# Masked softmax of a matmul: mask loaded ahead of W, zero fills on VectorE, row spread from the identity on ScalarE, TensorE busy on zeros until data lands

## The chip, the cores and the metric

The kernel runs on one core of one Trainium2 chip. The metric is the time of one execution on the device, in microseconds (us). The profile's span is shorter, because it runs from the first to the last instruction. How much shorter depends on the kernel: 1.8 us for the changed kernel (1.75 to 1.85 in its four runs), but 2.3 for the kernel before (median of 97 later runs, 2.18 to 2.47). So some 0.5 us of any difference between these two lies outside the span, where no profile shows its cause.

"Granted clock" is the share of full speed that TensorE was allowed, as the profile records it. x0, x1 and so on are the inputs of units 0, 1 and so on.

The records call a run "slow" when it is over 1.5% above the fastest run of the same kernel. Here that label is about time alone: among the later runs of the kernel before, one took 94.12 us at a mean granted clock of 0.973 and is called slow, another took 91.67 us at 0.972 and is called fast. The clock does not separate them. The profiled run of this kernel is a slow one (94.61 us, clock 0.957). The spread of the kernel before turns out to be part of the story.

## The reference

```python
batch, m, k, n = 16, 512, 512, 512
x = randn(batch, m, k); weight = randn(k, n); scale = 0.125      # float32
mask = (np.triu(np.ones((m, n))) == 0)                           # strictly lower triangle, as float32

y = scale * np.matmul(x, weight)
y = np.where(mask == 1, y, -1e9)
return softmax(y, axis=-1)
```

## The kernel before

Sixteen units of work, each of 1 MB of x in and 1 MB of output. A unit holds one half (upper or lower 256 rows) of two batches, four rows per partition. For each unit VectorE casts x to bf16, TensorE transposes it, VectorE and ScalarE bring the transposes back from PSUM, TensorE multiplies with W and adds a mask bias (`band`) through the identity, ScalarE takes the exponential with row sums, VectorE divides, and SyncE stores. For the upper half only 256 columns are computed, since the rest is masked; those output halves are filled once with constants.

The opening, which the change touches, prepares what all units use: W in bf16, the identity, the output fills, and the band, which is made from the diagonal blocks of the mask with a matrix `spread` that gives each mask row its place among the partitions.

```python
    load(0)                                               # 1 MB on SyncE's DMA queue
    seq(nc.sync.dma_start(w_f32, weight...))              # 1 MB
    seq(nc.sync.dma_start(diag_f32, diag_r))              # 0.26 MB in rows of 512 bytes
    for u in range(1, X_BUFS):                            # X_BUFS = 8
        load(u)
    make_identity(nc, ident_bf)                           # GpSimd
    nc.gpsimd.memset(spread, 0.0)
    # ... eight affine_selects on GpSimd set its ones ...
    # ... two memsets of band on GpSimd ...
    for i in range(0, OUT_BUFS, 2):
        nc.gpsimd.memset(ots[i][:, :, HB:], 0.0)          # 128 x 1024 float32 each
        nc.gpsimd.memset(ots[i][0:2, 0, HB:], 1.0 / N)
    cast(0); transpose(0); evict(0)
    # W: four casts of 128x512, two on VectorE, two on ScalarE
    # diag_bf = mask bias from diag_f32 (VectorE)
    # for t in range(4): matmul(spread, diag_bf), two copies into band (VectorE, ScalarE)
    cast(1)
    for u in range(U + 1):
        # transpose(u+1), cast(u+2), evict(u+1), multiply(u), normalise(u-1), store(u-1)
        # and then, behind that store in the same queue, load(u-1+X_BUFS)
```

All loads and stores go through one DMA queue, in this order. TensorE's program has the transposes of x1 ahead of the first multiply.

The softmax here doesn't subtract the row's maximum and nothing guards it: scores larger than these inputs give would overflow.

## Time and profile before

| | before |
|---|---|
| time, first comparison | 93.98 us median of 4 runs (93.84 to 94.58) |
| span of the profiled run | 92.3 us |
| TensorE / VectorE / ScalarE / GpSimd busy | 75 / 65 / 59 / 17% |
| DMA queue | 34.87 MB, 92.7% of 16 engines' span |
| steady TensorE work | 16.85 to 81.9 us |
| first store / last store issued | 25.63 / 84.57 us |

The page, the chain of waits and the windows of this kernel stand in the prediction below. One more view is useful: the groups of instructions, kept apart by shape. A line gives source line, engine, operation, what it writes and reads with shapes, number of instructions, then busy us and mean ns of one, then idle time before them.

```profile
L83 DVE CAST xb<-xf 128x2048 bf16<-128x2048 f32 x16 | 20.2, 1270 | 8.5 <-DMA xf<-in_x_dram 8.5
...
L185 POOL MEMSET ot<- 128x1024 f32 x4 | 4.6, 1185 | 0.1
...
L193 DVE CAST w_bf<-w_f 128x512 bf16<-128x512 f32 x2 | 3.1, 1612 | 0.0
```

A cast of W with 512 columns took 1612 ns, more than a cast of x with four times as many. The four large fills on GpSimd (POOL, named `ot`) ran beside it.

### The profile page before, as it was taken

How to read it: one execution, taken by the hardware profiler on the slowest of the kernel's cores; microseconds unless marked ns; L12 is line 12 of the kernel's file. 1: busy time of each engine (PE TensorE's matmuls, PEld its weight loads, DVE VectorE, ACT ScalarE, POOL GpSimd, SP SyncE). 2: the span in 40 equal slices, each digit the busy share in tenths (PEclk: the TensorE clock that was granted, in tenths of full speed). 3: DMA queues.
4: the chain of work that ended last, by engine and by line, in shares of the span. 5: the costliest groups of instructions: out<-in, count | busy, mean ns of one | idle time of the engine just before them, and what ended most of it. 6: DMA issues, size and time to landing. Idle time of an engine off the chain costs nothing.

```text
span 92.3 us, 1608 instructions
## 1 busy us (share of the span) xinstructions
PE 68.8 (75%) x580; PEld 48.7 (53%) x580; DVE 60.0 (65%) x119; ACT 54.4 (59%) x151; POOL 15.9 (17%) x33
## 2 busy tenths in 40 slices
PE   0005225699999999999999999999999999940000
PEld 0005100677659857956975885796598577510000
DVE  0045979950857995995999599599395977616000
ACT  5000716064868777977877788797787879650000
POOL 7999960000100010010001001000100010100000
PEclk9999999999999999999999999999999999997555
DMA  0889999999999999999999999999999999999930
GB/s 32 334 309 309 387 430 423 437 415 430 419 419 312 405 426 291 323 423 415 415 433 426 423 430 412 430 419 433 423 430 426 423 423 433 423 426 423 394 156 11
DMA packets 5670, 34.95 MB, mean 379 GB/s; under 512 B 544, under 2 KB 1056, under 8 KB 1568
## 3 DMA queue, kind: packets, MB, share of 16 engines
q1 hardware_dynamic: 5664, 34.87, 92.7%
q8 instruction: 4, 0.07, 0.3%
q14 instruction: 2, 0.02, 0.0%
HBM read 18.09 MB, written 16.78 MB: 378 GB/s over the span
## 4 chain that ended last, share of the span: by engine, by line
PE 72%; DVE 12%; DMA 5%; ACT 1%; DVEq 0%; issue 0%; ACTq 0%
PE py L116 47%; PE pt L92 17%; PE py L125 8%; DMA xf<-in_x_dram 5%; DVE xb L83 3%; DVE w_bf L193 3%; DVE band L216 2%; DVE ot L152 1%; DVE xt L102 1%; PE py L209 1%; ACT ot L135 1%; DVE diag_bf L197 1%; DVEq L263 0%; DVE rinv L150 0%; ACTq L263 0%
## 5 line engine op out<-in xcount | busy, mean ns | idle before, releaser
L116 PE MATMUL py<-w_bf,xt 128*128 128x256 bf16 (+1 forms) x256 | 51.4, 335 | 0.0
L135 ACT ACTIVATE ot<-py 128x256 f32<-128x256 f32 (+1 forms) x64 | 31.2, 493 | 9.3 <-PE py L125 9.1
L116 PEld LDWEIGHTS <-xt 128*128 128x128 bf16 x256 | 25.3, 101 | 12.6
L83 DVE CAST xb<-xf 128x2048 bf16<-128x2048 f32 x16 | 20.2, 1270 | 8.5 <-DMA xf<-in_x_dram 8.5
L92 PE MATMUL pt<-ident_bf,xb 128*128 128x128 bf16 x256 | 18.6, 231 | 9.6 <-DVE xb L83 9.6
L103 ACT COPY xt<-pt 128x1024 bf16<-128x1024 bf16 x16 | 16.2, 1012 | 15.5 <-PE pt L92 11.2
L152 DVE TENSOR_SCALAR ot<-ot,rinv 128x256 f32<-128x256 f32 (+1 forms) x64 | 23.5, 430 | 0.8
L92 PEld LDWEIGHTS <-xb 128*128 128x128 bf16 x256 | 17.0, 104 | 11.6 <-DVE xb L83 10.5
L102 DVE COPY xt<-pt 128x1024 bf16<-128x1024 bf16 x16 | 11.0, 689 | 11.3 <-PE pt L92 11.3
L125 PE MATMUL py<-band,ident_bf 128*128 128x256 bf16 x64 | 18.0, 282 | 0.0
L154 POOL MEMSET ot<- 2x256 f32 x8 | 3.6, 449 | 63.1 <-DVE ot L152 63.1
L135 ACT ACTIVATION_READ_ACCUMULATOR ot<-py 128x1 f32 x64 | 12.8, 200 | 0.0
L125 PEld LDWEIGHTS <-ident_bf 128*128 128x128 bf16 x64 | 6.5, 101 | 4.3
L150 DVE RECIPROCAL rinv<-rsum 128x4 f32<-128x4 f32 x16 | 2.7, 169 | 3.2 <-ACT ot L135 3.2
L185 POOL MEMSET ot<- 128x1024 f32 x4 | 4.6, 1185 | 0.1
L209 PE MATMUL py<-diag_bf,spread 128*128 128x512 bf16 x4 | 1.9, 620 | 3.5 <-DVE diag_bf L197 3.5
L173 POOL TENSOR_SCALAR_AFFINE_SELECT spread<-spread 128x64 bf16<-128x64 bf16 x8 | 3.2, 438 | 0.0
L193 DVE CAST w_bf<-w_f 128x512 bf16<-128x512 f32 x2 | 3.1, 1612 | 0.0
L216 ACT CAST band<-py 64x256 bf16<-64x256 f32 x4 | 1.5, 368 | 2.7 <-DVE band L216 2.5
L209 PEld LDWEIGHTS <-spread 128*128 128x128 bf16 x4 | 0.5, 136 | 4.2 <-POOL ot L186 3.7
L216 DVE CAST band<-py 64x256 bf16<-64x256 f32 x4 | 1.7, 416 | 0.7 <-PE py L209 0.7
L103 ACT ACT_TABLE_LOAD x1 | 1.3, 1283 | 0.7 <-PEq L249 0.7
(12 smaller groups left out, 6.8 us busy)
## 6 DMA issues: line engine op xcount, KB each, us to landing
xf<-in_x_dram SPq DMA_DIRECT2D x16, 1024.0 KB, 14.1
out_dram<-ot SPq DMA_DIRECT2D x16, 1024.0 KB, 11.0
w_f<-in_weight_dram SPq DMA_DIRECT2D x1, 1024.0 KB, 7.6
diag_f<-in_mask_dram SPq DMA_DIRECT2D x1, 256.0 KB, 8.3
```

Of the source, the lines that this page charges most:

```text
L83: seq(nc.vector.tensor_copy(xb, st_x.pop(u)))
L92: nc.tensor.transpose(st_pt[u][kt // 2][:, kt % 2, t], xb[:, t, kt * P : (kt + 1) * P], ident_bf,)
L102: seq(nc.vector.tensor_copy(xt[:, 0:2], pt[0]))
L103: seq(nc.scalar.copy(xt[:, 2:4], pt[1]))
L116: nc.tensor.matmul(py[:, :NC], lhsT=xt[:, kt, t], rhs=w_bf[:, kt, :NC], start=(kt == 0), stop=(kt == KT - 1),)
L125: nc.tensor.matmul(py[:, h * HB : NC], lhsT=ident_bf, rhs=band[:, h, t], start=False, stop=True, skip_group_check=True,)
L135: nc.scalar.activation(out=ot[:, t, :NC], in_=py[:, :NC], func=AF.Exp, bias=0.0, scale=float(scale), accum_out=rsum[:, t : t + 1],)
L152: seq(nc.vector.tensor_scalar_mul(ot[:, t, :NC], ot[:, t, :NC], rinv[:, t : t + 1]))
L154: seq(nc.gpsimd.memset(ot[0:2, 0, :HB], 1.0 / N))
L185: nc.gpsimd.memset(ots[i][:, :, HB:], 0.0)
L193: seq(nc.vector.tensor_copy(w_bf[:, kt], w_f32[:, kt]))
L216: seq(copy(band[half, :, t, g * P : (g + 1) * P], src[half, :, g]))
```

## The change

The intent is a shorter opening: the mask lands early so that its chain of small steps runs while W is still on its way, GpSimd is relieved of the fills and the row spread, and TensorE is kept at work on zeros so that its clock is up when data lands.

```diff
     load(0)
+    seq(nc.sync.dma_start(diag_f32, diag_r))
     seq(nc.sync.dma_start(w_f32, weight...))
-    seq(nc.sync.dma_start(diag_f32, diag_r))
 ...
+    nc.vector.memset(zeros, 0.0)
+    idle = psum_y.tile([P, N], FP32, name="py")
+    for _ in range(WARM):                                  # WARM = 12
+        seq(nc.tensor.matmul(idle, lhsT=zeros[:, :P], rhs=zeros, start=True, stop=True))
     make_identity(nc, ident_bf)
-    nc.gpsimd.memset(spread, 0.0)
-    # eight affine_selects on GpSimd
 ...
-        nc.gpsimd.memset(ots[i][:, :, HB:], 0.0)
+        nc.vector.memset(ots[i][:, :, HB:], 0.0)
 ...
+    # four ScalarE copies of 128x128: spread from ident_bf
     cast(0)
-    transpose(0); evict(0)
-    # four casts of W
     # diag_bf (VectorE)
+    transpose(0); evict(0)
     # spread matmuls and band copies
+    seq(nc.vector.tensor_copy(w_bf[:, 0:2], w_f32[:, 0:2]))
+    seq(nc.scalar.copy(w_bf[:, 2:4], w_f32[:, 2:4]))
     cast(1)
```

More of the change, by code (lines that the diff above doesn't have):

```diff
@@ L17 @@
 OUT_BUFS = 8
+WARM = 12
 @with_exitstack
@@ L69 @@
     spread = const.tile([P, T, P], BF16, name="spread")
+    zeros = const.tile([P, N], BF16, name="zeros")
     band = const.tile([P, 2, T, HB], BF16, name="band")
@@ L161 @@
     load(0)
+    seq(nc.sync.dma_start(diag_f32, diag_r))
     seq(nc.sync.dma_start(w_f32, weight.rearrange("(kt p) n -> p kt n", p=P)))
-    seq(nc.sync.dma_start(diag_f32, diag_r))
     for u in range(1, X_BUFS):
         load(u)
+    nc.vector.memset(zeros, 0.0)
+    idle = psum_y.tile([P, N], FP32, name="py")
+    for _ in range(WARM):
+        seq(nc.tensor.matmul(idle, lhsT=zeros[:, :P], rhs=zeros, start=True, stop=True))
     make_identity(nc, ident_bf)
-    nc.gpsimd.memset(spread, 0.0)
-    for t in range(T):
-        for g in range(2):
-            nc.gpsimd.affine_select(
-                out=spread[:, t, g * HP : (g + 1) * HP].rearrange("k (p e) -> k p e", e=2),
-                in_=spread[:, t, g * HP : (g + 1) * HP].rearrange("k (p e) -> k p e", e=2),
-                pattern=[[-4, HP // 2], [0, 2]],
-                base=-t,
-                channel_multiplier=1,
-                compare_op=ALU.not_equal,
-                fill=1.0,
-            )
     nc.gpsimd.memset(band[:HP, :, :, P:], MASK_NEG)
@@ L184 @@
     for i in range(0, OUT_BUFS, 2):
-        nc.gpsimd.memset(ots[i][:, :, HB:], 0.0)
+        nc.vector.memset(ots[i][:, :, HB:], 0.0)
         nc.gpsimd.memset(ots[i][0:2, 0, HB:], 1.0 / N)
-    cast(0)
-    transpose(0)
-    evict(0)
-    for kt in range(KT):
-        if kt % 2 == 0:
-            seq(nc.vector.tensor_copy(w_bf[:, kt], w_f32[:, kt]))
-        else:
-            seq(nc.scalar.copy(w_bf[:, kt], w_f32[:, kt]))
+    for g in range(2):
+        for e in range(2):
+            seq(
+                nc.scalar.copy(
+                    spread.rearrange("k t (g p e) -> k t g p e", g=2, e=2)[:, :, g, :, e],
+                    ident_bf.rearrange("k (p t) -> k t p", t=T),
+                )
+            )
+    cast(0)
     seq(
@@ L205 @@
     )
+    transpose(0)
+    evict(0)
     for t in range(T):
```

## The prediction

> **What bounds the kernel now.** I read the page first. No compute engine is busy for more than 75% of the span, but the DMA engines are full almost from the first microseconds to the end:
>
> ```profile
> span 92.3 us, 1608 instructions
> ...
> PE   0005225699999999999999999999999999940000
> ...
> DMA  0889999999999999999999999999999999999930
> ```
>
> So there are two long resources: TensorE, without a hole from about 17 to 82 us, and the DMA queue. Next I read the chain of waits in order of time (start, length, what):
>
> ```profile
> 5.82 2.07 DVE xb L83
> ...
> 9.70 3.06 DVE w_bf L193 x2
> ...
> 15.66 1.14 DVE xb L83
> ...
> 16.85 1.89 PE pt L92 x16
> ...
> 21.94 0.85 PE py L116 x4
> ...
> 23.88 0.86 PE py L116 x4
> ```
>
> From 5.8 to 16.85 us the chain is preparation, nearly all on VectorE: cast of x0, casts of W, mask bias, band, cast of x1. From there TensorE runs unbroken, but four matmuls of 256 columns take 0.85 us before 22.8 us, and four of 512 columns take 0.86 after: TensorE does its first 6 us at half speed. Third come windows of 1 us (busy time of PE, PEld, DVE, ACT and POOL, granted clock, DMA share, GB/s):
>
> ```profile
> 28.00:29.00 1.00, 1.00 (x17) 0.95 (x15) 0.74 (x2) 0.74 (x3) 0.00 (x0) 1.00 0.91 328
> 29.00:30.00 1.00, 1.00 (x11) 0.90 (x10) 0.96 (x4) 1.00 (x3) 0.00 (x0) 1.00 1.14 270
> ...
> 35.00:36.00 1.00, 1.00 (x14) 0.75 (x13) 0.00 (x1) 0.72 (x3) 0.00 (x0) 1.00 0.89 213
> ...
> 84.00:85.00 1.00, 0.00 (x0) 0.00 (x0) 0.54 (x2) 0.00 (x0) 0.00 (x0) 0.64 0.97 410
> ...
> 89.00:90.00 1.00, 0.00 (x0) 0.00 (x0) 0.00 (x0) 0.00 (x0) 0.00 (x0) 0.50 0.06 25
> ```
>
> The queue moves about 428 GB/s through most of the run, also after TensorE has ended at 81.9, so it still has work then. But it has weak spots: 28 to 30 us, and 35 to 39 us (213, 328, 279, 320). At the end it trails off for two microseconds at a share of 0.06, which is one sixteenth: a single one of the 16 DMA engines is still finishing. Last, the issues, window by window: what is issued when, and how long it takes to land. The first store, issued at 25.63, lands in 5.9 us; the last, issued at 84.57, in 6.7:
>
> ```profile
> out_dram<-ot SPq DMA_DIRECT2D x1, 1024.0 KB, 5.9
> ...
> out_dram<-ot SPq DMA_DIRECT2D x1, 1024.0 KB, 6.7
> ```
>
> Later stores take 11 to 15, because they stand behind a backlog. The first load, alone in the queue, took 5.0. So the queue was close to dry at 25.6, when the eight first loads were nearly done and the first store came, and again only just fed at 84.6. My reading: **TensorE's chain and the DMA queue are bound together**, and the queue is slightly the later of the two.
>
> **What the Trainium skill says.** "TensorE: Matmul & The Clock Gate", Part 1, says that the array runs at half clock until it has been busy for a free-running window of about 3.4 us, and falls back after an idle one. The trace agrees: 213 ns per 256 columns until 22.8, then 109, and 2.4 us after the last matmul the granted clock falls to 0.50. "SBUF — State Buffer", Who interferes with whom, says of the port pair that VectorE and GpSimd share that it is an exclusive lock and the loser of a conflict blocks. The trace fits: the cast of x0, beside GpSimd's fills, took 2.06 us against 1.21 to 1.23 for the later ones, and a cast of 128x512 of W took 1.61, though a quarter of the size of the x casts. "VectorE: DVE Perf Modes", Zero memsets can be issued as uint32, gives one cycle per element; no VectorE memset is in this trace. "DMA: Bandwidth & Descriptors", Where 436 GB/s comes from, puts the fabric at 435.2 GB/s; the trace's 410 to 442 per window sits there, so I expect no more than 428 on average.
>
> **The change, part by part.**
> - Fills. GpSimd loses the memset of the row spread, eight selects (3.2 us) and four large memsets (4 x 1.185 = 4.7 us). VectorE gains four memsets of 1024 columns: at one cycle per element, with the 0.96 GHz that the page gives VectorE, an estimate of 1.07 us each, 4.3 in all. They run from about 1 to 5.3 us, before x0 lands at 5.8, where VectorE was idle: no cost. With GpSimd quiet by then, the x0 cast should take 1.22 us and end near 7.0, not 7.9.
> - Mask before W. The mask is 0.26 MB behind x0; it took 1.3 us in the queue behind W (W landed at 9.1, the mask at 10.4). Now it should land near 7.3 and W at the 10.4 where the mask was. The bias (0.6 us), the eviction of the transposes (0.69) and the four band copies (4 x 0.42 = 1.7) then run from 7.4 to about 10.6, before W. One W cast of 128x1024, half an x cast, is 0.6 us: VectorE is free near 11.3. ScalarE has the other half, two times 0.57 = 1.1 us, done by about 12.
> - The new first wait. x1 stands behind the same 2.36 MB as before: issued at 2.64, landed 10.3 us later, at 12.9. The change does not move that. So cast of x1 at 12.9 to 14.1, transposes at 14.15 in place of 16.85: **TensorE's steady work starts 2.7 us earlier**, and no more, however quickly the opening is prepared.
> - Spread. Four ScalarE copies of 128x128 replace it, in the first 4 us, where ScalarE is idle: nothing on the path.
> - Twelve zero matmuls of 512 columns at half clock are 12 x 0.43 = 5.1 us, from about 1.1 to 6.2 us. The first transposes then run at full speed (0.9 us, not 1.9) and the row-spread matmuls too, but that lies ahead of the wait for x1. From about 9.5 to 14.15 TensorE is idle for some 4.6 us, and 2.4 were enough at the end of the trace for the clock to fall. So I expect it cold again at 14.15; the last transposes and the first multiply (5.9 us at half speed, 3.0 at full) gain only by the phase of the window, some 0.5 us on average and at most 2.9.
>
> TensorE therefore ends near 81.9 - 2.7 - 0.3 = 78.9, and the last store is issued near 81.6. If TensorE alone set the end, the gain would be 3 us.
>
> **What the queue makes of it.** It must move 34.87 MB: at 428 GB/s 81.5 us, from 2.4 us on. In the opening it loses 1.3 us to the gap at 5 us and to the 512-byte rows of the mask (windows of 199, 265 and 254 GB/s), which the change only reorders. That gives 85.2 for a queue that never starves. The trace shows its body ending at 88.5: 0.6 us is lost at 28 to 30, 1.3 at 35 to 39, 0.3 at 84 to 87, some 1.1 scattered. The single late engine then adds 2.8, to 91.3. Stores that start near 22.7, with three loads still ahead of them, keep the queue deep from then on. I count the 0.6 and the 0.3 as starvation that goes, half of the 1.3 (at 35 us over 2 MB were still outstanding, so it is not plain starvation), and a third of the 2.8, because the late engine seems to have fallen behind around those weak spots: by 27 us the windows add up to the 9.7 MB of all loads through x7, and yet x7, issued at 9.09, landed 20.2 us later at 29.3. Sum: 0.6 + 0.3 + 0.65 + 0.9 = 2.45 us. This is below TensorE's 3, so the queue keeps the last word. 93.99 - 2.45 = 91.5.
>
> **Rivals.**
> - The earlier work is hidden entirely. For it: the DMA share is near 1 in every window after 10 us, so the weak spots may be slow memory and not missing work, and would come again. Then only 0.3 to 0.9 us is gained: 93.1 to 93.7, "same".
> - TensorE's chain carries through in full, and it stays warm: 2.7 + 2.9 = 5.6, so 88.4. Against it: the queue would have to end at 85.7, close to the 85.2 of one without any loss.
> - The late engine vanishes with the starvation: body at 86.4, tail of 1 us, gain of 3.5 to 4, so 90. Possible, since I cannot tell why it is late.
> - Slower, because four VectorE memsets push the x0 cast back, or because last loads come later behind earlier stores. Even at GpSimd's 1.185 us the fills end by 5.9; and x1 leaves 1.6 us of slack. The last x waits on VectorE total only 2.7 us, and TensorE then still had earlier work. Unlikely.
>
> **Range and chances.** The middle is 91.5, with most of the doubt in how much of the weak spots and of the late engine goes: from the first rival's 93.3 to 90.0. The 2% line is at 92.1, a gain of 1.9, which is close to my middle; hence a good share for "same".
>
> **What would show it.** In the changed kernel: casts of x1 waiting for its load until about 12.9 and transposes at about 14.2; zero matmuls to about 6; matmuls of 256 columns still at 213 ns in the first multiply; first store issued at 22 to 23 us and landing in over 8 us rather than 5.9; no windows near 300 GB/s around 28; TensorE ended near 79 and the DMA still near 428 GB/s for 6 us after its last matmul. It is wrong if weak windows return at the same rate with a deep queue, if the single-engine tail stays at 2 us or more, or if the first multiply already runs at 109 ns and the end follows TensorE.

## The result

| | before | changed |
|---|---|---|
| time, median (range), 4 runs each | 93.98 (93.84 to 94.58) | 91.25 (91.14 to 91.26) |
| ratio of fast runs | | 0.9695, 95% interval 0.9653 to 0.9737 |
| span of the profiled run | 92.3 | 89.5 |
| transposes of x1 start | 16.85 | 14.53 |
| first store issued, landed after | 25.63, 5.9 us | 23.17, 8.9 us |
| last matmul ends / last store issued | 81.9 / 84.57 | 79.45 / 82.11 |
| last landing | 91.3 | 88.5 |

Ratios are the mean time of one kernel's fast runs over that of the other's fast runs in the same rounds, so not quite the ratio of the medians (91.25 / 93.98 = 0.971). The changed kernel is faster by 3% in this comparison. The four runs of the kernel before were all in the slower part of what this kernel does: in 97 later runs it took 91.52 to 94.79 us (median 93.91), and only 28 of them stayed below 92.9. Against its best runs the gain is about 0.3 us, so what the change removes is mostly the slow runs. And of the 2.7 us between the medians, about 0.5 lies outside the span (1.8 against 2.3 us), which leaves about 2.2 for the windows to explain.

The page of the changed kernel, with the rows for TensorE, its granted clock and the DMA engines:

```profile
span 89.5 us, 1610 instructions
...
PE   4997205999999999999999999999999999950000
...
PEclk9999995559999999999999999999999999997555
DMA  0959999999999999999999999999999999999960
```

TensorE is busy on zeros from the start, then idle in slices 5 and 6, and its clock falls to half just before the steady work begins (13.4 and 14.5 us). In the kernel before this row showed full clock from 17 to 22 us, although four matmuls of 256 columns took the same 0.85 us there; the durations of the matmuls are the safer reading. The chain of waits (start, length, what):

```profile
2.63 10.59 DMA xf<-in_x_dram
13.23 0.02 issue
13.25 1.24 DVE xb L85
14.49 0.05 issue
14.53 1.89 PE pt L94 x16
...
18.55 0.85 PE py L118 x4
...
22.39 0.86 PE py L118 x4
```

The whole preparation has left the chain; one wait for the load of x1 stands in its place. Four matmuls of 256 columns still take 0.85 us at 18.55, and four of 512 take 0.86 at 22.39. The windows (columns as in the prediction; the last two are DMA share and GB/s):

```profile
6.00:7.00 1.00, 0.50 (x2) 0.00 (x0) 1.00 (x1) 0.00 (x0) 0.00 (x0) 1.00 0.35 80
...
28.00:29.00 1.00, 1.00 (x18) 0.97 (x16) 1.00 (x2) 0.90 (x5) 0.00 (x0) 1.00 1.03 434
29.00:30.00 1.00, 0.95 (x9) 0.53 (x8) 1.00 (x3) 0.64 (x1) 0.00 (x0) 1.00 1.02 426
...
35.00:36.00 1.00, 1.00 (x12) 0.90 (x10) 1.00 (x3) 1.00 (x6) 0.00 (x0) 1.00 0.99 418
...
84.00:85.00 1.00, 0.00 (x0) 0.00 (x0) 0.00 (x0) 0.00 (x0) 0.00 (x0) 0.50 1.01 426
...
87.00:88.00 1.00, 0.00 (x0) 0.00 (x0) 0.00 (x0) 0.00 (x0) 0.00 (x0) 0.50 0.20 82
```

The weak windows of 28 to 30 and 35 to 39 us are gone: from 8 to 86 us no window is below 393 GB/s. The queue still moves 426 GB/s five microseconds after the last matmul, then trails off until the last landing at 88.5. A new hole stands at 6 us, where the mask's 512-byte rows now move. Last, the first and the last store in the list of issues (KB, us from issue to landing):

```profile
out_dram<-ot SPq DMA_DIRECT2D x1, 1024.0 KB, 8.9
...
out_dram<-ot SPq DMA_DIRECT2D x1, 1024.0 KB, 6.4
```

The first store takes 8.9 us to land, behind loads, where it took 5.9 before. Bytes issued less bytes moved, an estimate from the issue times and the windows, says how much work was left when that store was issued: 0.5 MB before, 1.7 MB now.

The difference of 2.8 us between the spans of the two traced runs can be read from the windows (the traced run of the kernel before, 94.61 us, is 0.6 above the median). At 428 GB/s the low last window of the body puts its end at 88.5 before and at 86.4 now (188 GB/s in the window from 86); that is 2.0 us. The tail behind it, to the last landing, was 2.8 and is 2.1 us; that is 0.7.

### The profile page after: what moved, and what is told of

The parts are those of the page before. It is cut to its first block, busy times and chain, and to the rows that moved or that the text cites. A ratio compares the mean times of both kernels' runs of the same rounds, so it can differ in the third digit from the quotient of the medians.

```text
span 89.5 us, 1610 instructions
## 1 busy us (share of the span) xinstructions
PE 71.9 (80%) x584; PEld 49.3 (55%) x592; DVE 60.5 (68%) x123; ACT 55.3 (62%) x154; POOL 7.3 (8%) x20
## 4 chain that ended last, share of the span: by engine, by line
PE 72%; DMA 12%; DVE 3%; SPq 2%; issue 1%; ACT 1%; DVEq 0%; ACTq 0%
PE py L118 48%; PE pt L94 16%; DMA xf<-in_x_dram 12%; PE py L127 8%; DVE ot L154 1%; DVE xb L85 1%; SPq L80 1%; ACT ot L137 1%; SPq L164 1%; SPq L165 1%; DVEq L264 0%; DVE rinv L152 0%; ACTq L264 0%
## 5 line engine op out<-in xcount | busy, mean ns | idle before, releaser
L118 PEld LDWEIGHTS <-xt 128*128 128x128 bf16 x256 | 25.3, 101 | 12.7
L85 DVE CAST xb<-xf 128x2048 bf16<-128x2048 f32 x16 | 19.5, 1221 | 6.2 <-DMA xf<-in_x_dram 6.2
L94 PE MATMUL pt<-ident_bf,xb 128*128 128x128 bf16 x256 | 17.7, 225 | 5.7 <-DVE xb L85 5.7
L94 PEld LDWEIGHTS <-xb 128*128 128x128 bf16 x256 | 16.2, 101 | 8.2 <-DVE xb L85 7.1
L156 POOL MEMSET ot<- 2x256 f32 x8 | 3.6, 449 | 67.8 <-DVE ot L154 67.8
L173 PE MATMUL py<-zeros 128*128 128x512 bf16 x12 | 5.3, 632 | 1.2 <-DVE zeros L170 1.2
L179 DVE MEMSET ot<- 128x1024 f32 x4 | 3.6, 912 | 0.6 <-issue 0.6
L173 PEld LDWEIGHTS <-zeros 128*128 128x128 bf16 x12 | 1.7, 145 | 3.9 <-issue 2.7
L180 POOL MEMSET ot<- 2x256 f32 x4 | 1.2, 302 | 1.5 <-DVE ot L179 1.4
L208 PE MATMUL py<-diag_bf,spread 128*128 128x512 bf16 x4 | 1.0, 377 | 0.2 <-DVE diag_bf L194 0.2
```

Of the source, the lines that this page charges most:

```text
L85: seq(nc.vector.tensor_copy(xb, st_x.pop(u)))
L94: nc.tensor.transpose(st_pt[u][kt // 2][:, kt % 2, t], xb[:, t, kt * P : (kt + 1) * P], ident_bf,)
L118: nc.tensor.matmul(py[:, :NC], lhsT=xt[:, kt, t], rhs=w_bf[:, kt, :NC], start=(kt == 0), stop=(kt == KT - 1),)
L156: seq(nc.gpsimd.memset(ot[0:2, 0, :HB], 1.0 / N))
L173: seq(nc.tensor.matmul(idle, lhsT=zeros[:, :P], rhs=zeros, start=True, stop=True))
L179: nc.vector.memset(ots[i][:, :, HB:], 0.0)
```

## The experiments

**My theory**: the DMA queue sets the end. VectorE's casts, held up by GpSimd's fills, started TensorE late, so the first stores came when the queue had almost no work left (0.5 MB, half a load); the time lost there was never made up. **Rivals**: TensorE's chain sets the end and gained from the earlier start and the warm clock; the weak windows belong to the memory and have nothing to do with the stores; each part of the change gives its share.

A word on the comparisons. The kernel before was run again with each set of experiments, and its spread is wide and without a clear gap: 91.67 to 94.76 (median 94.17, 23 runs) beside the first four, 91.52 to 94.65 (median 93.67, 39 runs) beside the next four, 91.67 to 94.65 (median 93.91, 23 runs) beside the two after these and 92.08 to 94.79 (median 93.59, 12 runs) beside the last two. The changed kernel was not run again, and the sets ran on three different chips, so that differences of half a microsecond between sets are not certain. Its few fast-labelled runs are the lower end of this spread, and the ratio of fast runs (0.98 to 0.99 for kernels at 91.2, verdict "unclear" in each case; 0.996, "same", for the run with ten loads) compares with that end alone. I therefore give medians and ranges of all runs. The changed kernel and those that behave like it stay within 0.3 us of their median, except where said. The one trace of the kernel before is of a run of 94.61 us, near its slow end; none of a run near 91.6 was taken. What the weak windows cost is thus read from that end, and the evidence for their cause is in kernels changed on purpose, not in the label.

### Without the zero matmuls

```diff
-    for _ in range(WARM):
+    for _ in range(0):
```

> The changed kernel without its twelve zero matmuls. If the wait for x1 (landed at 13.2 us) hides the whole opening, as predicted: the first transposes take 1.9 us in place of 1.07, the band is ready a microsecond later, transposes of x1 still start at 14.5, time 91.2 +- 0.2. If the zero matmuls earn something on the path: 0.5 to 1 us slower, 91.8 to 92.2.

Measured: 91.19 us (91.08 to 91.22, 4 runs). The first transposes took 1.89 us in place of 1.07, the four row-spread matmuls 1.91 in place of 1.02, and the transposes of x1 started at 14.54. The zero matmuls earn nothing: what they hurry is over before x1 lands in any case, VectorE with 1.25 us to spare. Without them TensorE even ended some 1.1 us earlier than in the changed kernel (78.3), because the array reached full speed earlier in the first multiply (at about 18 us, not 20), and the last store was issued at 81.0. The time stayed the same.

### TensorE kept busy until x1

```diff
+    idle2 = psum_y.tile([P, N], FP32, name="py")
+    for _ in range(22):
+        seq(nc.tensor.matmul(idle2, lhsT=zeros[:, :P], rhs=zeros, start=True, stop=True))
     seq(nc.vector.tensor_copy(w_bf[:, 0:2], w_f32[:, 0:2]))
```

> The changed kernel with 22 more zero matmuls between the row spread and the transposes of x1, so that TensorE does not fall back to half clock. The first multiply then runs at full speed and TensorE ends some 2.5 to 2.9 us earlier, near 76.8. If the DMA queue sets the end: time 91.0 to 91.3 all the same. If TensorE's chain sets it: 88.4 to 88.8.

Measured: 91.20 us (90.97 to 91.22, 4 runs). The row of the granted clock stays at full until the work ends:

```profile
PEclk9999999999999999999999999999999999997555
```

The first multiply ran at 109 ns per 256 columns, and the chain of waits ends TensorE's part at

```profile
77.05 0.12 PE py L127
```

which is 2.3 us earlier than in the changed kernel (79.45), and the last store is issued at 79.83 in place of 82.11. The time does not move. This is the test that TensorE's chain fails: 2.3 us off it are worth nothing, because the last store then stands behind that much more work in the queue: it takes 8.5 us to land in place of 6.4.

### Only the fills moved, on the kernel before

```diff
-        nc.gpsimd.memset(ots[i][:, :, HB:], 0.0)
+        nc.vector.memset(ots[i][:, :, HB:], 0.0)
```

> The kernel before with one edit: the four large zero fills on VectorE in place of GpSimd. If GpSimd's fills slowed VectorE's casts: cast of x0 1.2 us, casts of W 0.35 to 0.4 us in place of 1.6, cast of x1 at 12.9 to 13.2, transposes of x1 near 14.3, time 91.3 +- 0.4, nearly the whole gain. If the gain is spread over all parts of the change: 92.8 to 93.5.

Measured: 91.22 us (91.04 to 91.47, 4 runs), the whole gain from one line of the kernel. The group of W's casts:

```profile
L193 DVE CAST w_bf<-w_f 128x512 bf16<-128x512 f32 x2 | 0.8, 420 | 0.0
```

1612 ns have become 420, with nothing changed but what GpSimd does at that time. The transposes of x1 started at 14.71. The cast of x0 was a partial miss: it still took 1.85 us, while GpSimd was busy with the row spread and the band until 6.85.

### VectorE held up on purpose, in the changed kernel

```diff
+    for _ in range(4):
+        seq(nc.vector.memset(pad, 0.0))
     cast(1)
```

> The changed kernel with four dummy VectorE memsets (4 x 1.07 us) ahead of the cast of x1, so that TensorE's steady work starts near 17.0 us, as in the kernel before, with all else as changed. If the earlier start, through earlier stores, is the whole gain: first store near 25.8 landing in 5 to 6.5 us, windows below 350 GB/s at 28 to 39 us again, time 93.5 to 94.1. If the weak windows are the memory's own, or the gain came from elsewhere: 91.5 to 92.2.

Measured: 93.55 us, median of 20 runs, 92.07 to 94.45; the kernel before in the same rounds 94.17, 91.67 to 94.76. Steady TensorE work began at 17.22, the first store was issued at 25.89 and landed in 5.9 us. The profiled run, 93.67 us, has the weak windows again:

```profile
29.00:30.00 1.00, 1.00 (x12) 0.90 (x10) 0.96 (x4) 0.98 (x2) 0.00 (x0) 1.00 1.25 311
...
35.00:36.00 1.00, 1.00 (x10) 0.64 (x9) 0.26 (x1) 0.71 (x3) 0.00 (x0) 1.00 0.91 262
...
37.00:38.00 1.00, 1.00 (x11) 0.89 (x10) 0.96 (x5) 1.00 (x2) 0.00 (x0) 1.00 0.98 262
```

All parts of the change are in place here except its effect on when TensorE begins, and with that effect most of the gain goes and the wide spread comes back. In the span all of it goes: the median is 91.7 us here, 91.8 for the kernel before in the same rounds and 89.45 for the changed kernel. The fast runs say the same (ratio 1.004 to the kernel before, 95% interval 0.998 to 1.011).

### Fills back on GpSimd, in the changed kernel

```diff
-        nc.vector.memset(ots[i][:, :, HB:], 0.0)
+        nc.gpsimd.memset(ots[i][:, :, HB:], 0.0)
```

> The changed kernel with one part undone: the four large fills back on GpSimd. If what counts is only that the preparation ends before x1 lands (1.8 us of slack): casts of x0 and W slower than 1.23 and 0.69 us, but transposes of x1 within 0.5 us of 14.5, time 91.2 to 91.7. If the fills are what the gain needs: 93 or more.

Measured: 91.29 us (91.16 to 91.31, 4 runs). The cast of x0 took 2.60 us, worse than before; but GpSimd, free of the row spread, was done at 9.2 us, before W landed, so W's cast took 0.67 and the transposes of x1 started at 14.58. The fills alone suffice, and the rest without the fills suffices too: each brings the preparation under the same wait.

### Only the mask first, on the kernel before

```diff
+    seq(nc.sync.dma_start(diag_f32, diag_r))
     seq(nc.sync.dma_start(w_f32, weight...))
-    seq(nc.sync.dma_start(diag_f32, diag_r))
```

> The kernel before with only the order of the mask and W loads swapped, all computing in its old order. VectorE then waits for W to about 10.4 before it casts it, still beside GpSimd's fills: transposes of x1 at 17 to 18 us, time 94.0 to 95.0. If the mask's place by itself helps: 93 or less.

Measured: median 93.12 us of 20 runs, 91.77 to 94.94, with 93.67 (91.52 to 94.65) for the kernel before: no clear change. My detail missed: the transposes of x1 started at 16.85, as before, not later. VectorE's casts of W were held until 12.7 us by GpSimd's fills in both orders, which hides when W lands. The first store was issued at 24.96, earlier by 0.7, for a reason not looked into.

### x1 ahead of mask and W

```diff
     load(0)
+    load(1)
     seq(nc.sync.dma_start(diag_f32, diag_r))
     seq(nc.sync.dma_start(w_f32, weight...))
-    for u in range(1, X_BUFS):
+    for u in range(2, X_BUFS):
```

> The changed kernel with x1 loaded before mask and W. TensorE then does not wait for x1 but for W, and the first multiply starts near 12.5 in place of 16.2. If the queue sets the end, only what the new order saves of the queue's weak opening (1.6 us lost between 5 and 8 us) counts: 90.3 to 91.3. If TensorE's chain sets it: 87.5 to 88.5.

Measured: 91.30 us (91.07 to 91.47, 4 runs). There is no gap behind x0 now, but the hole moves along with the mask: half-microsecond windows from 8.0 to 9.5 us show 68, 160 and 52 GB/s. x0, x1, mask and W have all landed at 13.3 us, as the same four had at 13.2 in the changed kernel, so the order of the loads changes nothing for the queue. The expected early start was a miss: W came that late, so TensorE's steady work began at 15.21, 0.7 us after the changed kernel's. The time is the same all the same.

### Two more loads in flight, on the kernel before

```diff
-X_BUFS = 8
+X_BUFS = 10
```

> The kernel before with ten x buffers in place of eight, so two more loads stand in the queue before the first store; computing unchanged. If the weak windows were a queue short of work: none below 380 GB/s at 28 to 39 us, the last x lands earlier, TensorE ends at 81.9 as before and the last store is issued at 84.6; it can then not land before some 89, time 91.3 to 92.5. If the weak windows are the memory's own: 93.6 to 94.2.

Measured: 91.78 us, median of 20 runs, 91.52 to 92.19; the kernel before in the same rounds 93.67, 91.52 to 94.65. The opening is untouched: W's casts take 3.15 us together, TensorE's steady work starts at 16.86, the first store is issued at 25.18. It takes 11.4 us to land, behind the added loads, and the weak windows are gone:

```profile
29.00:30.00 1.00, 1.00 (x11) 0.90 (x10) 1.00 (x4) 1.00 (x6) 0.00 (x0) 1.00 1.04 434
...
35.00:36.00 1.00, 1.00 (x19) 0.99 (x18) 0.34 (x1) 0.69 (x2) 0.00 (x0) 1.00 0.99 418
...
37.00:38.00 1.00, 1.00 (x12) 0.89 (x10) 1.00 (x3) 1.00 (x6) 0.00 (x0) 1.00 1.05 442
```

A constant changed from 8 to 10 gives most of the gain and takes away the spread. The memory is not slow at these times by itself; it needs work in the queue. In the span this is the whole gain: the median is 89.5 us, as in the changed kernel, and the last landing is at 88.5 in both. The 0.5 us that are missing to 91.2 lie outside the span, where this kernel has the 2.3 us of the kernel before. TensorE's late end shows all the same: the queue runs short from 83 to 86 us (336, 131 and 320 GB/s) before the last store, issued at 84.12, which lands in 4.4 us against 6.4. Behind the body there is then only a tail of 0.8 us.

### Half as late

Three dummy memsets in place of four.

> The changed kernel with three dummy memsets ahead of the cast of x1 (four in the run with a late x1): TensorE's steady work about 1.4 us later than changed, 1.1 us earlier than before; first store near 24.7. If lateness costs in proportion, 92.3 to 92.7. If only a queue that runs dry costs: the first store still finds the last of the eight loads moving (they end near 25.6[...]), so it is near the edge: either 91.2 to 91.6 with a tight spread, or a wide spread from 91.3 to 94.

Measured: 91.22, 91.45, 92.28 and 92.97 us. The traced run, 91.45, issued its first store at 23.86 and shows no weak window. This fits the edge that was expected: of four runs of one kernel, two are close to the changed kernel, one loses 1 us and one 1.7. Only the fast one was traced.

The same estimate of bytes issued but not yet moved can be made for these seven traced runs, at the moment when the first store of each was issued:

| run | work left, MB | lowest window from 26 to 40 us, GB/s |
|---|---|---|
| mask and W on ScalarE's queue (below) | 0.0 | 0 |
| kernel before | 0.5 | 213 |
| VectorE held up | 0.6 | 262 |
| only the mask first | 1.0 | 270, one window only |
| half as late (this run) | 1.5 | 377 |
| changed | 1.7 | 393 |
| ten loads | 2.8 | 393 |

In these seven traces the weak windows go with the work left at that moment, and not with the work in the queue when they occur: at 35 us, in its weakest window, the kernel before had 3.2 MB outstanding, and the changed kernel moved 418 GB/s there with 3.0.

### The last store spread unevenly

```diff
-    seq(nc.sync.dma_start(out_r[u // 2, u % 2], ...))        # for the last unit:
+    seq(nc.sync.dma_start(out_r[...][0:56], ot[0:112] ...))
+    seq(nc.sync.dma_start(out_r[...][56:64], ot[112:128] ...))
```

> The changed kernel with its last store in two pieces: rows of 56 of the 64 row groups, then the other 8, so that the last megabyte is spread unevenly over the 16 DMA engines (two of them get none of it, if engines go by blocks of row groups). In the changed kernel one or two engines finish some 1.5 us after the rest. If they are those relieved: last landing near 87.5, time 90.2 to 90.6. If they are among those that get more: 91.6 to 92. If neither: 91.2.

Measured: 91.97 us (91.81 to 92.56, 20 runs), slower by 0.7. The trace shows the queue thin out from 84 us on, over 4 us, where it was full to 86 in the changed kernel. This fits engines that got more bytes and end later, which they would do whether they were late before or not, so it does not tell which engines were the late ones. Nor were they one or two, as I had read: the share at 86.5 to 87.5 us in the changed kernel (about 0.3) is that of some five engines. This closes one way of shortening the tail; which engines are late, and why, stays open.

### The mask on ScalarE's DMA queue

```diff
-    seq(nc.sync.dma_start(diag_f32, diag_r))
+    seq(nc.scalar.dma_start(diag_f32, diag_r))
```

> The changed kernel with the mask load issued by ScalarE, on its own DMA queue, in place of SyncE's second place. In every order tried the windows in which the mask's 512-byte rows move show the engines at a third of their share, about 1.1 us lost in all. If the queue's time is the bound and the other queue's bytes fill these holes: x1 lands 0.5 to 1.1 us earlier, all landings after it too, time 90.2 to 90.8. If the holes stay (the engines are slow on small rows, whatever the queue): 91.1 to 91.4.

Measured: 91.75 us (91.63 to 91.81, 7 runs), slower by 0.5, outside both expectations. (These rounds ran on another chip, where the kernel before did not come below 92.08, so the size is uncertain; the trace is not.) The hole does not fill; it moves to the very start. The windows from 2 to 4 us fall to 93 and 133 GB/s, x0 lands in 8.1 us in place of 5.0, and with it everything behind it is late.

### Mask and W on ScalarE's DMA queue

The same edit for W too.

> The changed kernel with both mask and W on ScalarE's queue, all x loads on SyncE's. If holes are filled as in the run with the mask alone, and the gap after x0 too: 90.0 to 90.6. x0 then shares the engines with mask and W and lands later than 5.8, which should cost nothing, because TensorE has slack. If two queues only share what one had: 91.1 to 91.4.

Measured: 96.29 us (95.32 to 97.10, 6 runs), the slowest of all. W shares the engines with a stream of x loads and lands 18.2 us after its issue; its cast starts at 19.38, TensorE's steady work at 21.27 and the first store at 29.84. All loads are long done by then, and the queue is plainly empty:

```profile
27.00:28.00 1.00, 1.00 (x19) 0.99 (x18) 0.32 (x1) 0.47 (x2) 0.00 (x0) 1.00 0.26 107
28.00:29.00 1.00, 0.95 (x7) 0.52 (x6) 0.96 (x4) 0.87 (x1) 0.09 (x1) 1.00 0.09 16
29.00:30.00 1.00, 1.00 (x7) 0.49 (x5) 1.00 (x4) 0.79 (x3) 0.35 (x1) 1.00 0.00 0
```

It was meant as an improvement and became a clear picture of an empty queue: TensorE works at full rate in these windows, and nothing moves. Weak windows follow here too after the first stores (262 and 287 GB/s from 33 to 35 us, 229 to 336 from 39 to 43). As a test of what sets the end it says less, because TensorE also ended 6.7 us later (86.1), which alone could account for the time.

No kernel of the study beats the changed one by more than its spread. Six very different openings (without zeros, with many zeros, fills alone, all but the fills, x1 early, and the change itself) end at 91.2 to 91.3 us.

## Why the prediction was right

The prediction was 91.5 us, 90.0 to 93.3; measured 91.25.

- **The first wait moves to x1.** Right, except that x1 was said to stay where it was. VectorE waits for x1, the transposes start at 14.53 (predicted 14.15), TensorE's work starts 2.3 us earlier (predicted 2.7). The difference is the sentence that the change does not move x1: it landed at 13.2, not 12.9. By 13 us the windows add up to 3.71 MB, against 3.78 before; the mask's small rows right behind x0 leave a wider hole (80 GB/s in the window at 6 us).
- **Fills and preparation are off the path.** Right. The four VectorE memsets ran 912 ns each, 1.07 us from start to start (estimated 1.07), and ended at 5.4, before x0 landed; the x0 cast took 1.23 us (predicted 1.22). Mask and W landed some 0.3 to 0.6 us later than estimated, hidden by the wait for x1.
- **Zero matmuls buy nothing.** Right, and tested: full clock for the first transposes, half again from 13.4 to 20.2 us, no effect on the time (91.19 without them, 91.20 with 22 more). Two details are loose. The text gives 0.5 us on average for the phase of the clock and then counts 0.3. And it says that the trace agrees with the window that it quotes. The clock fell 2.4 us after the last matmul before the change and 2.2 after it, but 4.0 us into the idle stretch of the changed opening (9.4 to 13.4). The direction agrees; one fixed length does not come out.
- **The queue keeps the last word.** Right, and tested most directly: TensorE done 2.3 us earlier still, and no change.
- **The sum of 2.45 us.** That the total is close to the measured 2.7 is partly luck. The terms were read from one traced run, at 94.61 us, and taken off a median of 93.99; between the traced runs the span shrank by 2.8 us, between typical runs by about 2.2, with 0.5 more outside the span that no term had. The terms, in the traced pair: of the 0.6, 1.3 and 0.3 in the weak windows I counted half of the 1.3 as incurable, because over 2 MB were still outstanding at 35 us. All of it went. After the queue has been nearly empty it loses time some microseconds later as well, and the run with ten loads shows that more work ahead of the first store cures both. On the other side the opening got some 0.2 us worse, where I had called it a mere reordering.
- **The late engine.** The size was nearly right (0.9 predicted, 0.7 measured). The tail is still 2.1 us, and the prediction had named a single-engine tail of 2 us or more as a sign of being wrong. By its length this sign came, although some five engines share the tail now. The reason that I gave is also weak: I read the late landing of x7 at 29.3 as a mark of starvation, and in the changed kernel x7 lands at 29.5, 21.6 us after its issue, with no weak window anywhere. Part of that lateness is there in any case.
- **Rivals.** The first (the weak windows are the memory's own and come again) fell with the ten loads. The second (TensorE's chain carries through) fell with the busy TensorE. The hope of a tail of 1 us did not come true; it is 2.1. "Slower" did not happen: the fills were over before x0 landed.

What stays open: why packets are slow in the weak windows, and again some microseconds later (the engines were not idle then: their busy share was 0.83 to 1.14 in the weak windows of the kernel before); what makes some engines late; and what the 0.5 us outside the span are. That the wide spread of the kernel before comes from how close each run gets to an empty queue fits the run with three memsets and the run with ten loads, but I have no trace of one of its own fast runs.

## What to carry to other kernels

When one queue carries all loads and stores and is nearly full, count its bytes first; then look for the moment at which the first loads run out and the first store is not yet there, because time lost at that point was not made up here. An earlier start of compute is worth what it does for that moment and nothing beyond, and a few more loads in flight can do the same with one constant. Fills on GpSimd beside casts on VectorE are not free work on an idle engine: look at the casts' durations, not at the fills'.

## What the Trainium skill lacked or had wrong

- "DMA: Bandwidth & Descriptors", Specifications, gives a minimum transfer for line rate of 512 bytes or more. The mask's rows are 512 bytes, and the windows in which they move show down to 80 GB/s in the changed kernel and 254 in the kernel before (windows of 1 us), and 52 with x1 ahead of them (0.5 us), against 410 to 442 with rows of 8 KB. That the size of the rows is the cause was not tested with other sizes.
- The same page, Where 436 GB/s comes from, says that the HBM side, about 358 GB/s per core, binds transfers between HBM and SBUF, although it adds that a load of 16 MB measured 425. With one core at work, loads and stores mixed moved 393 to 451 GB/s per window for nearly 80 us in the changed kernel, so 358 did not bind here.
- The same page, Issuing engines are not separate DMA queues, says that DMAs of several engines interleave on the same 16 DMA engines, and that issuing from several only saves the sequencer's time to issue. It does not say that the interleaving can cost time: with the mask on ScalarE's queue x0 landed 8.1 us after its issue in place of 5.0, and W on that queue landed after 18.2 us in place of 8.7.
- No page has it that a queue once short of work can be slow again later: windows of 213 to 344 GB/s from 35 to 39 us with over 2 MB issued and outstanding, in the two traced runs whose first store met 0.5 to 0.6 MB, and run-to-run spreads of 2.4 to 3.3 us for these two kernels in place of 0.1 to 0.7.
- "SBUF — State Buffer", Who interferes with whom, explains the block between VectorE and GpSimd but gives no size for fills: a 128x512 cast took 1612 ns beside GpSimd memsets and 420 ns without them.
